# A two-layer transformer trunk: sixteen weight-sum transfers and the masks issued later, and the transposes of the second token half issued in two pieces with a free order

## The chip, the cores and the metric

The kernel runs on one core of one Trainium2 chip. The metric is device time in microseconds for one whole execution, as the median over the timed runs. The core has a matrix engine (PE, with its weight loads counted apart as PEld), a vector engine (DVE), a scalar engine (ACT), GpSimd (POOL) and a synchronisation engine (SP) that issues most transfers; POOL issues the rest. Each engine works through its own instructions in the order in which they stand in its queue, and waits where the next one lacks an operand or a buffer.

## The reference, cut to what matters

The input is 1024 tokens of 1024 channels in fp32. Each of two layers is: a SwiGLU feed-forward block (FFN) with half weight, a token mixer, a second FFN with half weight. Each block has an RMSNorm on its input and one on its output.

```
def swiglu(x, wg, wu, wd):
    return (jax.nn.silu(x @ wg) * (x @ wu)) @ wd
...
for layer in range(DEPTH):                       # DEPTH = 2
    f = swiglu(rmsnorm(h, ffn_pre_g[layer, 0]), ...)      # D_FF = 1408
    h = h + 0.5 * rmsnorm(f, ffn_post_g[layer, 0])
    m = rmsnorm(h, mix_pre_g[layer])
    m = hybrid_mixer(m, ...) if layer % 2 == 0 else stick_breaking(m, ...)
    h = h + rmsnorm(m, mix_post_g[layer])
    f = swiglu(rmsnorm(h, ffn_pre_g[layer, 1]), ...)
    h = h + 0.5 * rmsnorm(f, ffn_post_g[layer, 1])
```

## The kernel before, in words

**Stages.** `build` runs six stages in a row: the FFNs and mixers of layer 0, then those of layer 1. The four FFNs are called L0F0, L0F1, L1F0 and L1F1 here, by layer and position. Tokens are handled in two halves of 512 (`TB`). Every fp32 operand is split into a rounded high part (a cast on ACT) and a rest (a subtraction on DVE), and a product is three matmuls per 128-row block, `mm3`: high weight by high data, high weight by data rest, weight rest by high data (lines 287, 288, 289). The third of them is the first to need DVE's half of the weight split.

**The gate loop.** `gu` computes gate and up with a Strassen scheme on 2x2 blocks. Its first loop runs over the 11 column blocks c of the gate weight. For each c it loads a 128-column tile (`load_w`, tile `rawt`), splits it into two quarters `wq` (`split_w`, ACT line 336 and DVE line 337), multiplies the first quarter with the first token half (`pa`, 12 matmuls), copies that to `ph` on ACT (line 434), and later, in `a12`, adds the second quarter's 12 matmuls into the same `pa` and applies Silu (ACT, line 414). The list `second` holds the products whose second quarter is still to come.

**The second token half.** Beside the gate loop `second_half(part)` brings in the second token half: `make_raw` transposes normed tokens into `xps` (line 327, four 128x128 transposes to a tile, one from each of the four token tiles `fx`, `fo1` or `xn`) and ACT evicts them to `xr` (line 329). Four parts of two tiles each go with c = 2 to 5. `combos(j)`, with c = 4 to 7, makes the Strassen sums of them on DVE (lines 388 to 397, seven operations and three splits each). The normed tokens come from `epilogue(1, ...)` of the stage before; its last steps, on DVE, ACT and POOL in turn, are the row scales `rs` (line 234) and the scaled rows (line 248).

**The up loop.** The second loop of `gu` runs over the same 11 c with five products of 12 matmuls (`pb`, `pc`, `pd`, `pc`, `pd`). `blocks(c)` loads one gate and one up tile and makes the block differences on POOL (lines 421 to 424), which ACT and DVE then split.

**Jobs.** Strassen sums of weights that later stages need are made in DRAM by transfers that POOL issues, sixteen to a set (`Blocks.sums`, line 82): `vsum` for the mixer's value projection, `wsum` for its output projection, `dsum` for the FFN's down projection. A set is four rounds that each wait for the round before. `job(loop)` issues a few per c. In L0F0 the gate loop has the mixer's masks (`mask_steps`, lines 163 to 187) and the `vsum` set, the up loop has `dsum` and `wsum`.

**Order.** A planner sets each engine's order from its own estimate of times. Instructions given to `keep_in_program_order` (here `pin`) stay in the order of the code among themselves. The gate loop's matmuls with c below 6 and the transposes of `second_half` are pinned, and so are the jobs on POOL.

**The down stage.** `down_strassen` follows with products `da`, `db`, `dc`, `de`, `dd`; its differences on POOL are lines 715 and 725. Then come `epilogue(0, ...)`, whose `rs` are POOL's next work, `make_x` for the first token half (line 268), and `epilogue(1, ...)`. The mixer's `values` first reads `vsum` as tile `rawd`.

Of the kernel before, what the change touches and what calls it, by code (L numbers as in the profile page):

```python
# [19 lines left out]
P = 128  # L20
D = 1024
S = 1024
KD = D // P
DFF = 1408
NF = DFF // P
# [28 lines left out]
class Blocks:  # L54
# [15 lines left out]
    def sums(self, T):  # L70

        dma = self.t.nc.gpsimd.dma_start
        pin = self.t.tc.keep_in_program_order
        T1, T2, T3, T4 = (T[n] for n in (1, 2, 3, 4))
        h = slice(0, self.KH * P // 2), slice(self.KH * P // 2, self.KH * P)
        steps = []
        for dst, src, add in ((T1, self.block(0, 0), None), (T3, self.block(0, 1), None),
                              (T1, self.block(0, 1), 1), (T3, self.block(1, 1), 1), (T2, T1, None),
                              (T2, self.block(1, 1), 1), (T4, T2, None), (T4, self.block(1, 0), 1)):
            for i in h:  # L80
                def step(dst=dst, src=src, add=add, i=i):
                    pin(dma(out=dst[i], in_=src[i], accum_op=ALU.add) if add else dma(out=dst[i], in_=src[i]))
                steps.append(step)
        return steps
# [5 lines left out]
class Trunk:  # L90
# [192 lines left out]

    def mm3(self, ps, ah, al, bh, bl, first, last, more=False):
        nc = self.nc
        pin = self.pin_mm or (lambda i: i)
        pin(nc.tensor.matmul(ps, lhsT=ah, rhs=bh, start=first, stop=False, skip_group_check=more))  # L287
        pin(nc.tensor.matmul(ps, lhsT=ah, rhs=bl, start=False, stop=False, skip_group_check=more))  # L288
        pin(nc.tensor.matmul(ps, lhsT=al, rhs=bh, start=False, stop=last, skip_group_check=more))  # L289


    def load_cols(self, w, c0, n):
# [24 lines left out]
        return ps  # L317


    def make_raw(self, xns, gname, gi, pool, order=range(KD), pin=lambda i: i):  # L320

        nc = self.nc
        res = {}
        for k in order:
            ps = self.tp.tile([P, TB], F32, name="xps", tag="tp")
            for t in range(NTT):
                pin(nc.tensor.transpose(ps[:, t * P:(t + 1) * P], xns[t][:, k * P:(k + 1) * P], self.ident))
            r = pool.tile([P, TB], F32, name="xr", tag="xr")
            nc.scalar.activation(out=r, in_=ps, func=AF.Copy, scale=self.col(gname, gi * KD + k))
            res[k] = r  # L330
        return res
# [22 lines left out]
    def gu(self, cx, wg, wu, A, xn1, gname, gi, jobs, begun):  # L354


        nc = self.nc
# [3 lines left out]
        xr = self.dyn(raw, "xr", KD)  # L361
        R = {}
# [1 line left out]
        rows = {}  # L364

        def second_half(part):
            R.update(self.make_raw(xn1, gname, gi, xr, [part, part + 4], pin))
            if part < 3:
                return
            self.hctx.close()  # L370
            self.foctx.close()
            rows["sx"] = self.dyn(s4, "sx", 4, side="right")
            rows["t2"] = self.dyn(s4, "t2p", 2, side="right")
# [8 lines left out]
        def combos(j):  # L382

            a21, a22 = R[j], R[j + 4]
            hi = lambda k: A[k][:, 0].bitcast(F32)
            lo = lambda k: A[k][:, 1].bitcast(F32)
            s1 = xr.tile([P, TB], F32, name="s1", tag="s1", bufs=1)
            tt(out=s1, in0=a21, in1=a22, op=ALU.add)
            stile(1, s1)
            tt(out=a21, in0=hi(j), in1=a21, op=ALU.subtract)  # L390
            tt(out=a21, in0=a21, in1=lo(j), op=ALU.add)
            stile(3, a21)
            tt(out=s1, in0=s1, in1=hi(j), op=ALU.subtract)
            tt(out=s1, in0=s1, in1=lo(j), op=ALU.subtract)
            stile(2, s1)
            tt(out=a21, in0=hi(j + 4), in1=s1, op=ALU.subtract)
            tt(out=a21, in0=a21, in1=lo(j + 4), op=ALU.add)

        ph, second = [], []
        pin = self.tc.keep_in_program_order  # L400
        paces = 3, -(-len(jobs[1]) // NF)

        def job(loop):
            for f in jobs[loop][:paces[loop]]:
                f()
            del jobs[loop][:paces[loop]]


        def a12():

# [14 lines left out]
            return {"t1": b11, "t2": t2, "t3": b12, "t4": b21, "b22": b22}  # L425

        for c in range(NF):

            self.pin_mm = pin if c < 6 else None
            h = [self.ph.tile([P, TB], F32, name="ph%d" % tb, tag="ph") for tb in range(2)]  # L430
            w0, w1 = begun if begun and c == 0 else self.gate_weights(wg, c)
            ps = self.acc.tile([P, TB], F32, name="pa", tag="acc")
            self.quarter(ps, w0, A[0:4], True, True)
            nc.scalar.copy(out=h[1], in_=ps)
            while len(second) > (c < 8):
                a12()
            second.append((ps, w1, h))
            ph.append(h)
            if 2 <= c <= 5:
                second_half(c - 2)  # L440
            if 4 <= c <= 7:
                combos(c - 4)
            if c > 2:
                job(0)

        B = blocks(0)
        W = [self.split_w(B[n]) for n in ("t2", "t3")]
# [8 lines left out]
        for c in range(NF):  # L456
# [10 lines left out]
            last = c == NF - 1  # L467
# [26 lines left out]
            tt(out=h[1], in0=c21, in1=c22, op=ALU.mult)  # L494
            if c > NF // 2:
                self.down_sums(ph, c - 1 - NF // 2)
            job(1)
        tmp.close()
        s4.close()
        return ph  # L500
# [110 lines left out]
    def ffn(self, l, f, x0, xn1, hsrc, hdst, last):  # L611
        a = self.a
        wg, wu, wd = a["ffn_w_gate"][l, f], a["ffn_w_up"][l, f], a["ffn_w_down"][l, f]
        cx = ExitStack()
        self.ph = self.dyn(cx, "ph", 2 * NF)
        self.s1 = []

        sums = lambda *sets: [step for steps in zip(*[B.sums(T) for B, T in sets]) for step in steps]
        down = self.down_blocks(l, f), self.wd[l, f]
        jobs = [], []  # L620
        if l + f == 0:
            jobs = self.mask_steps() + sums((self.value_blocks(0), self.tv)), sums(down, (self.out_blocks(0), self.td))
        elif l == 0:
            jobs = [], sums(down, (self.value_blocks(1), self.tv))
        elif f == 0:
            jobs = [], sums(down)
        ph = self.gu(cx, wg, wu, x0, xn1, "ffn_pre_g", 2 * l + f, jobs, self.begun_w)
        self.open_fo()
        pg = self.load_pg(a["ffn_post_g"][l, f])
        nxt = ("mix_pre_g", l) if f == 0 else ("ffn_pre_g", 2 * (l + 1))  # L630
        r = self.down_strassen(wd, self.wd[l, f], ph, pg, hsrc, hdst, None if last else nxt)
        cx.close()
        self.hctx.close()
        return r
# [13 lines left out]
        gt(out=z, in0=x, in1=z, op=ALU.subtract)  # L648
        self.s1.append(s1)

    def down_strassen(self, w, T, ph, pg, hsrc, hdst, nxt):
        nc = self.nc
        tt = nc.vector.tensor_tensor
        gt = nc.gpsimd.tensor_tensor
# [68 lines left out]
            tt(out=u2[t], in0=pb[t], in1=u2[t], op=ALU.add)  # L723
        for j in range(KH):
            gt(out=ph[j + KH][0], in0=ph[j][0], in1=ph[j + KH][0], op=ALU.subtract)

        cp = [pair("c22") for _ in range(2)]
        c22 = [cp[t // 2][:, t % 2] for t in range(NTT)]
# [917 lines left out]
    def build(self):  # L1646
# [15 lines left out]
            self.normed(h, h)  # L1662
        src = a["x"][0]
        n = 0
        self.begun_w = self.pin_mm = None
        stages = [(l, step) for l in range(2) for step in ("f0", "mix", "f1")]
        firsts = [(lambda l=l: self.row_weights(lambda j: self.value_blocks(l).src(j, 0))) if step == "mix" else
                  (lambda l=l, f=int(step[1]): self.gate_weights(a["ffn_w_gate"][l, f], 0)) for l, step in stages]
# [43 lines left out]
```

## Time and profile before

| | |
|---|---|
| time, median of 3 runs | 2486.64 us (2486.34 to 2493.13) |
| time of the profiled execution | 2488.17 us |
| its span | 2486.2 us |
| PE busy | 2352.8 us, 95% of the span, 11165 matmuls and transposes |
| DVE, ACT, POOL busy | 1840.1, 1141.2, 723.4 us |
| mean clock granted to PE | 0.985 of full speed |

The profile is one execution. "Busy" counts an engine's own work, not its waits; "idle before" an instruction, with what released it, is where an engine's waits show. In the timeline a row has the start, the duration, the engine, line, operation, tiles and shapes, and in brackets the idle time just ahead of it. Matmul durations overlap: in a run of matmuls the distance between two starts is what counts.

### The profile page before, as it was taken

The numbers are of one execution on the slowest core, as the hardware profiler recorded it, in microseconds if no ns is written. First come the engines' busy times: TensorE is split into PE (matmuls) and PEld (weight loads), VectorE is DVE, ScalarE is ACT, GpSimd is POOL, SyncE is SP. The second block draws the span as 40 slices with busy tenths as digits, with TensorE's granted clock in tenths as the row PEclk, the third lists the DMA queues.
The fourth block names the chain that finished last, engine by engine and source line by source line (L and its number), as shares of the span: only waits on it lengthen the run. The fifth ranks groups of instructions, "written<-read, shape, count | busy, mean of one in ns | idle before, by whom it ended". The sixth has DMA issues, their size and how long they took to land. (4 is left out here: it accounts for less than half of the span.)

```text
span 2486.2 us, 31734 instructions
## 1 busy us (share of the span) xinstructions
PE 2352.8 (95%) x11165; PEld 1925.0 (77%) x11165; DVE 1840.1 (74%) x2877; ACT 1141.2 (46%) x2285; POOL 723.4 (29%) x729
## 2 busy tenths in 40 slices
PE   7999999999888898999989999999999999799998
PEld 6778877777677776877768878778888878588886
DVE  7768789387577778678688677785767677786777
ACT  6323456332466666423456225463333345652343
POOL 3547210011011111567022563110332430234520
PEclk9999999999999998999999999999999999899999
DMA  8867444411112463767454743355574244532234
GB/s 240 229 154 187 141 148 155 143 52 68 60 60 77 150 222 108 194 151 180 140 184 125 162 118 123 122 167 180 126 185 104 90 131 163 176 85 76 73 110 170
DMA packets 278407, 343.64 MB, mean 138 GB/s; under 512 B 13972, under 2 KB 190312, under 8 KB 277736
## 3 DMA queue, kind: packets, MB, share of 16 engines
q1 hardware_dynamic: 251352, 261.39, 33.6%
q0 software_dynamic: 26896, 80.22, 14.2%
q8 instruction: 88, 1.44, 0.2%
q14 instruction: 71, 0.58, 0.1%
HBM read 292.28 MB, written 124.78 MB: 168 GB/s over the span
## 5 line engine op out<-in xcount | busy, mean ns | idle before, releaser
L234 POOL TENSOR_TENSOR rs<-ms,nhalf 128x1 f32<-128x1 f32 (+1 forms) x136 | 103.7, 769 | 839.6 <-DVE ms L232 728.7
L336 ACT CAST wq<-rawt 128x512 fp32r<-128x512 f32 x264 | 163.3, 622 | 362.6 <-PE pc L289 181.9
L337 DVE TENSOR_TENSOR wq<-rawt,wq 128x512 fp32r<-128x512 f32 x264 | 246.5, 938 | 41.9 <-ACT wq L336 37.9
L276 ACT CAST hl<-rawd 128x512 fp32r<-128x512 f32 x212 | 130.7, 620 | 212.0 <-PE dc L289 63.9
L277 DVE TENSOR_TENSOR hl<-rawd,hl 128x512 fp32r<-128x512 f32 x212 | 155.4, 737 | 81.6 <-ACT hl L276 81.5
L287 PE MATMUL pps<-hl,wh 128*128 128x512 f32 x512 | 209.3, 409 | 1.4 <-ACT k L966 1.2
L288 PE MATMUL pps<-hl,wh 128*128 128x512 f32 x512 | 203.6, 398 | 0.0
L289 PE MATMUL pps<-hl,wl 128*128 128x512 f32 x512 | 202.9, 396 | 0.0
L421 POOL TENSOR_TENSOR rawt<-rawt 128x512 f32<-128x512 f32 x44 | 65.7, 1494 | 342.7 <-DMA rawt<-in_ffn_w_up_dram 287.0
L287 PE MATMUL pa<-hl,wq 128*128 128x512 f32 x352 | 143.1, 407 | 5.8 <-ACT wq L336 3.2
L289 PE MATMUL pa<-hl,wq 128*128 128x512 f32 x352 | 141.0, 401 | 8.1 <-DVE wq L337 8.1
L287 PE MATMUL pc<-hl,wq 128*128 128x512 f32 x336 | 133.0, 396 | 12.7 <-DVE c L472 11.8
L288 PE MATMUL pa<-hl,wq 128*128 128x512 f32 x352 | 140.5, 399 | 0.0
L289 PE MATMUL pc<-hl,wq 128*128 128x512 f32 x336 | 133.3, 397 | 0.0
L288 PE MATMUL pc<-hl,wq 128*128 128x512 f32 x336 | 133.3, 397 | 0.0
L288 PE MATMUL pd<-hl,wq 128*128 128x512 f32 x336 | 131.3, 391 | 0.0
L289 PE MATMUL pd<-hl,wq 128*128 128x512 f32 x336 | 131.2, 391 | 0.0
L287 PE MATMUL pd<-hl,wq 128*128 128x512 f32 x336 | 131.1, 390 | 0.0
L1076 DVE TENSOR_TENSOR_SCAN a<-a,zero 128x128 f32<-128x128 f32 (+3 forms) x64 | 90.2, 1409 | 46.5 <-POOL a L1073 46.2
L983 PE MATMUL z<-k,q 128*128 128x512 f32 (+2 forms) x480 | 113.6, 361 | 9.5 <-ACT k L966 4.3
L287 PEld LDWEIGHTS pps<-hl,wh 128*128 128x128 f32 x512 | 97.7, 191 | 21.5 <-ACT k L966 2.6
L289 PEld LDWEIGHTS pps<-hl,wl 128*128 128x128 f32 x512 | 97.5, 191 | 21.1
(359 smaller groups left out, 6642.0 us busy)
## 6 DMA issues: line engine op xcount, KB each, us to landing
rawt<-in_ffn_w_gate_dram SPq DMA_DIRECT2D x88, 512.0 KB, 4.0
dsum<-in_ffn_w_down_dram POOLq DMA_DIRECT2D x48, 640.0 KB, 8.0
rawt<-in_ffn_w_up_dram SPq DMA_DIRECT2D x44, 512.0 KB, 4.2
rawd<-dsum SPq DMA_DIRECT2D x80, 256.0 KB, 2.7
hres<-h SPq DMA_DIRECT2D x40, 512.0 KB, 2.7
h<-hres SPq DMA_DIRECT2D x40, 512.0 KB, 4.6
rawd<-in_ffn_w_down_dram SPq DMA_DIRECT2D x76, 256.0 KB, 2.7
dsum<-dsum POOLq DMA_DIRECT2D x16, 640.0 KB, 5.7
```

What stands on the lines that cost most here:

```text
L234: nc.gpsimd.tensor_tensor(out=rs, in0=ms, in1=self.nhalf.to_broadcast([P, n]) if n > 1 else self.nhalf, op=ALU.pow)
L276: nc.scalar.copy(out=t[:, 0], in_=src)
L277: nc.vector.tensor_tensor(out=t[:, 1], in0=src, in1=t[:, 0].bitcast(F32), op=ALU.subtract)
L287: pin(nc.tensor.matmul(ps, lhsT=ah, rhs=bh, start=first, stop=False, skip_group_check=more))
L288: pin(nc.tensor.matmul(ps, lhsT=ah, rhs=bl, start=False, stop=False, skip_group_check=more))
L289: pin(nc.tensor.matmul(ps, lhsT=al, rhs=bh, start=False, stop=last, skip_group_check=more))
L336: nc.scalar.copy(out=w[:, 0], in_=src)
L337: nc.vector.tensor_tensor(out=w[:, 1], in0=src, in1=w[:, 0].bitcast(F32), op=ALU.subtract)
L421: gt(out=b11, in0=b12, in1=b11, op=ALU.subtract)
L983: nc.tensor.matmul(z[:, :wide], lhsT=lhs[:, i * P:(i + 1) * P], rhs=rhs[:, c0:c0 + wide], start=j == 0, stop=j == len(passes) - 1 and not ...
L1076: nc.vector.tensor_tensor_scan(out=ra, data0=ra, data1=self.zero1.to_broadcast([P, n]), initial=1.0, op0=ALU.mult, op1=ALU.add)
```

## The change

Three edits in one:

1. In L0F0 the sixteen `vsum` transfers and the masks leave the gate loop. They are handed to `down_strassen` as `steps` and issued there behind POOL's last difference, transfers first and masks behind them. The gate loop has no jobs any more; the up loop's jobs are the same ones at the same pace.
2. In all four FFNs `second_half` comes in two parts of four tiles (c = 3 and 4) in place of four parts of two (c = 2 to 5), and `combos` goes with c = 5 to 8 in place of 4 to 7; the last `pa` drains one c later.
3. Nothing on PE in the gate loop is pinned, so that the planner orders these matmuls and transposes.

```
 def mm3(self, ps, ah, al, bh, bl, first, last, more=False):
-    pin = self.pin_mm or (lambda i: i)
-    pin(nc.tensor.matmul(ps, lhsT=ah, rhs=bh, ...))      # and the two others
+    nc.tensor.matmul(ps, lhsT=ah, rhs=bh, ...)
...
 def second_half(part):
-    R.update(self.make_raw(xn1, gname, gi, xr, [part, part + 4], pin))
-    if part < 3:
+    R.update(self.make_raw(xn1, gname, gi, xr, [2 * part, 2 * part + 4, 2 * part + 1, 2 * part + 5]))
+    if not part:
         return
...
-    self.pin_mm = pin if c < 6 else None
...
-    while len(second) > (c < 8):
+    while len(second) > (c < 9):
         a12()
...
-    if 2 <= c <= 5:
-        second_half(c - 2)
-    if 4 <= c <= 7:
-        combos(c - 4)
-    if c > 2:
-        job(0)
+    if c in (3, 4):
+        second_half(c - 3)
+    if 5 <= c <= 8:
+        combos(c - 5)
...
 if l + f == 0:
-    jobs = self.mask_steps() + sums((self.value_blocks(0), self.tv)), sums(down, (self.out_blocks(0), self.td))
+    jobs = sums(down, (self.out_blocks(0), self.td))
+    steps = sums((self.value_blocks(0), self.tv)) + self.mask_steps()
...
 # down_strassen
     for j in range(KH):
         gt(out=ph[j + KH][0], in0=ph[j][0], in1=ph[j + KH][0], op=ALU.subtract)
+    for f in steps:
+        f()
```

The work itself is unchanged: every engine has the same instructions, and SP's queue has the same order. What moves is the order on PE, ACT and DVE inside the four gate loops, and on POOL in L0F0.

PE in L0F1 (L1F1 has the same pattern), where the second token half comes in; `fo1_0` to `fo1_3` are its four normed token tiles, `pa` are gate products. Before:

```order
L288 MATMUL pa_8511<-hl_8383,wq_8423 128x512
L289 MATMUL pa_8511<-hl_8383,wq_8423 128x512
L327 MATMUL xps_8586<-ident_98,fo1_0_8386 128x128
L327 MATMUL xps_8586<-ident_98,fo1_1_8387 128x128
L327 MATMUL xps_8586<-ident_98,fo1_2_8388 128x128
L327 MATMUL xps_8586<-ident_98,fo1_3_8389 128x128
L327 MATMUL xps_8593<-ident_98,fo1_0_8386 128x128
```

And after:

```order
L288 MATMUL pa_8596<-hl_8351,wq_8590 128x512
L326 MATMUL xps_8623<-ident_98,fo1_0_8386 128x128
L326 MATMUL xps_8630<-ident_98,fo1_0_8386 128x128
L326 MATMUL xps_8637<-ident_98,fo1_0_8386 128x128
L326 MATMUL xps_8644<-ident_98,fo1_0_8386 128x128
L286 MATMUL pa_8661<-hl_8327,wq_8655 128x512
L287 MATMUL pa_8661<-hl_8327,wq_8655 128x512
L326 MATMUL xps_8623<-ident_98,fo1_1_8387 128x128
L326 MATMUL xps_8630<-ident_98,fo1_1_8387 128x128
L326 MATMUL xps_8637<-ident_98,fo1_1_8387 128x128
L326 MATMUL xps_8644<-ident_98,fo1_1_8387 128x128
L288 MATMUL pa_8661<-hl_8327,wq_8655 128x512
```

Before, 48 gate matmuls stand between the stage's first `pa` and the first transpose, and that transpose's tile needs all four token tiles at once. After, 75 stand there, and the transposes go by token tile, with 2, 3 and 4 matmuls between the tiles.

PE at the start of L0F0; `wq_310` and `wq_313` are the two quarters of gate block c = 0, `wq_334` the first quarter of c = 1, `pa_316` and `pa_340` their products. Before:

```order
L289 MATMUL pa_316<-hl_244,wq_310 128x512
L287 MATMUL pa_340<-hl_235,wq_334 128x512
L288 MATMUL pa_340<-hl_235,wq_334 128x512
L289 MATMUL pa_340<-hl_235,wq_334 128x512
L287 MATMUL pa_340<-hl_238,wq_334 128x512
```

And after:

```order
L288 MATMUL pa_316<-hl_244,wq_310 128x512
L286 MATMUL pa_316<-hl_247,wq_313 128x512
L287 MATMUL pa_316<-hl_247,wq_313 128x512
L288 MATMUL pa_316<-hl_247,wq_313 128x512
L286 MATMUL pa_316<-hl_250,wq_313 128x512
L287 MATMUL pa_316<-hl_250,wq_313 128x512
L288 MATMUL pa_316<-hl_250,wq_313 128x512
L286 MATMUL pa_316<-hl_253,wq_313 128x512
L286 MATMUL pa_340<-hl_235,wq_334 128x512
L287 MATMUL pa_340<-hl_235,wq_334 128x512
L287 MATMUL pa_316<-hl_253,wq_313 128x512
```

The second quarter of c = 0 now begins ahead of block c = 1, and the two interleave.

POOL in L0F0, where the `vsum` set ends and the up loop's first block follows (`vsum_135` is the last of the four sums). Before:

```order
L82 DMA vsum_135<-vsum_133 16x8192 x2
L82 DMA vsum_135<-in_hyb_w_in_dram 256x512 x2
L421 TENSOR_TENSOR rawt<-rawt 128x512
L422 TENSOR_TENSOR t_890<-rawt 128x512
L423 TENSOR_TENSOR rawt<-rawt 128x512
L424 TENSOR_TENSOR rawt<-rawt,t_890 128x512
L82 DMA dsum_1_140<-in_ffn_w_down_dram 320x512
```

And after, in the down stage:

```order
L720 TENSOR_TENSOR ph_746<-ph_456,ph_746 128x512
L82 DMA vsum_132<-in_hyb_w_in_dram 256x512 x2
L82 DMA vsum_134<-in_hyb_w_in_dram 256x512 x2
L82 DMA vsum_132<-in_hyb_w_in_dram 256x512 x2
L82 DMA vsum_134<-in_hyb_w_in_dram 256x512 x2
L82 DMA vsum_133<-vsum_132 16x8192 x2
L82 DMA vsum_133<-in_hyb_w_in_dram 256x512 x2
L82 DMA vsum_135<-vsum_133 16x8192 x2
L82 DMA vsum_135<-in_hyb_w_in_dram 256x512 x2
L168 MEMSET zero_2407 128x1
```

The block differences of c = 0 now stand right behind the input norms' `rs`, and the set stands behind the last difference of the down stage, ahead of the masks and of `epilogue(0)`'s `rs`.

More of the change, by code (lines that the diff above doesn't have):

```diff
@@ L285, in mm3 @@
         nc = self.nc
-        pin = self.pin_mm or (lambda i: i)
-        pin(nc.tensor.matmul(ps, lhsT=ah, rhs=bh, start=first, stop=False, skip_group_check=more))
-        pin(nc.tensor.matmul(ps, lhsT=ah, rhs=bl, start=False, stop=False, skip_group_check=more))
-        pin(nc.tensor.matmul(ps, lhsT=al, rhs=bh, start=False, stop=last, skip_group_check=more))
+        nc.tensor.matmul(ps, lhsT=ah, rhs=bh, start=first, stop=False, skip_group_check=more)
+        nc.tensor.matmul(ps, lhsT=ah, rhs=bl, start=False, stop=False, skip_group_check=more)
+        nc.tensor.matmul(ps, lhsT=al, rhs=bh, start=False, stop=last, skip_group_check=more)
     def load_cols(self, w, c0, n):
@@ L317, in proj, with make_raw @@
         return ps
-    def make_raw(self, xns, gname, gi, pool, order=range(KD), pin=lambda i: i):
+    def make_raw(self, xns, gname, gi, pool, order=range(KD)):
         nc = self.nc
@@ L326, in make_raw @@
             for t in range(NTT):
-                pin(nc.tensor.transpose(ps[:, t * P:(t + 1) * P], xns[t][:, k * P:(k + 1) * P], self.ident))
+                nc.tensor.transpose(ps[:, t * P:(t + 1) * P], xns[t][:, k * P:(k + 1) * P], self.ident)
             r = pool.tile([P, TB], F32, name="xr", tag="xr")
@@ L399, in gu, with job @@
         ph, second = [], []
[L400 to L404, printed above, removed]
+        pace = -(-len(jobs) // NF)
+        def job():
+            for f in jobs[:pace]:
                 f()
-            del jobs[loop][:paces[loop]]
+            del jobs[:pace]
         def a12():
@@ L496, in gu @@
                 self.down_sums(ph, c - 1 - NF // 2)
-            job(1)
+            job()
         tmp.close()
@@ L619, in ffn @@
         down = self.down_blocks(l, f), self.wd[l, f]
-        jobs = [], []
+        jobs, steps = [], []
         if l + f == 0:
-            jobs = self.mask_steps() + sums((self.value_blocks(0), self.tv)), sums(down, (self.out_blocks(0), self.td))
+            jobs = sums(down, (self.out_blocks(0), self.td))
+            steps = sums((self.value_blocks(0), self.tv)) + self.mask_steps()
         elif l == 0:
-            jobs = [], sums(down, (self.value_blocks(1), self.tv))
+            jobs = sums(down, (self.value_blocks(1), self.tv))
         elif f == 0:
-            jobs = [], sums(down)
+            jobs = sums(down)
         ph = self.gu(cx, wg, wu, x0, xn1, "ffn_pre_g", 2 * l + f, jobs, self.begun_w)
@@ L630, in ffn @@
         nxt = ("mix_pre_g", l) if f == 0 else ("ffn_pre_g", 2 * (l + 1))
-        r = self.down_strassen(wd, self.wd[l, f], ph, pg, hsrc, hdst, None if last else nxt)
+        r = self.down_strassen(wd, self.wd[l, f], ph, pg, hsrc, hdst, None if last else nxt, steps)
         cx.close()
@@ L649, in down_sums, with down_strassen @@
         self.s1.append(s1)
-    def down_strassen(self, w, T, ph, pg, hsrc, hdst, nxt):
+    def down_strassen(self, w, T, ph, pg, hsrc, hdst, nxt, steps):
         nc = self.nc
@@ L1664, in build @@
         n = 0
-        self.begun_w = self.pin_mm = None
+        self.begun_w = None
         stages = [(l, step) for l in range(2) for step in ("f0", "mix", "f1")]
```

## The prediction

> **What bounds the kernel now.** I read the busy times first, then PE's list of waits, then the timeline where those waits lie.
>
> ```profile
> PE 2352.8 (95%) x11165; PEld 1925.0 (77%) x11165; DVE 1840.1 (74%) x2877; ACT 1141.2 (46%) x2285; POOL 723.4 (29%) x729
> ```
>
> PE is the bound, and the work on it is unchanged. An edit can win time only from PE's idle time, 133.4 us of the span of 2486.2 (2486.2 less 2352.8), and from stretches in which matmuls run slowly. PE's longest waits, over the whole program (us in all, times, longest):
>
> ```profile
> PE xps L327 <- DVE ms L232: 16.7, 6, 5.6
> PE pc L287 <- DVE c L472: 11.8, 7, 4.4
> PE pa L289 <- DVE wq L337: 8.1, 3, 5.5
> ```
>
> All three are in loops that the change reorders. The first is the entry of the second token half in L0F1 and L1F1. PE's timeline in L0F1 (start, us):
>
> ```profile
> 949.64 0.39 PE L289 MATMUL pa<-hl,wq 128*128 128x512 f32 x1
> 955.67 0.45 PE L327 MATMUL xps<-ident,fo 128*128 128x128 f32 x1 [5.64 <-DVE ms L232]
> 957.44 0.48 PE L327 MATMUL xps<-ident,fo 128*128 128x128 f32 x1 [1.32 <-DVE ms L232]
> 959.29 0.47 PE L327 MATMUL xps<-ident,fo 128*128 128x128 f32 x1 [1.38 <-DVE ms L232]
> 961.15 1.33 PE L327 MATMUL xps<-ident,fo 128*128 128x128 f32 x5 [1.38 <-DVE fo L248]
> 962.13 0.78 PE L287 MATMUL pa<-hl,wq 128*128 128x512 f32 x1
> ...
> 965.97 0.40 PE L287 MATMUL pa<-hl,wq 128*128 128x512 f32 x1
> ```
>
> The 48 gate matmuls are used up at 949.64; then PE stands before four transposes, each waiting for one more normed token tile: 5.64 + 1.32 + 1.38 + 1.38 = 9.72 us. The nine matmuls from 962.13 to 965.97 take 3.84 us, 0.427 each, where undisturbed ones start 0.2275 apart (949.64 closes an undisturbed run): 1.8 us more. So 11.5 us go here. The three waits on `ms` are 8.34 us, and twice that is the 16.7 of the whole program, so L1F1 loses as much.
>
> **Edits 2 and 3 in L0F1 and L1F1.** DVE's rows that make the four tiles ready, the first and the last of the four (the two between start at even distances of 1.85):
>
> ```profile
> 954.78 0.75 DVE L248 TENSOR_SCALAR fo<-h,rs 128x1024 f32<-128x1024 f32 x1
> 960.34 0.75 DVE L248 TENSOR_SCALAR fo<-h,rs 128x1024 f32<-128x1024 f32 x1 [0.44 <-POOL rs L234]
> ```
>
> The tiles are ready at 955.53, 957.38, 959.23 and 961.09, and DVE's order ahead of them stays. The changed order has 75 matmuls ahead of the first transpose, 27 more: 949.87 + 27 x 0.2275 = 956.0. Each tile then feeds four transposes (0.1 us each, from the eight in 0.8 us that start at 35.30, below). Tile 0 finds no wait; 2 matmuls later, at 956.9, PE waits 0.5 for tile 1; after 3 more 0.7 for tile 2; after 4 more 0.6 for tile 3. PE ends at 961.5 with 84 matmuls and 16 transposes done. Before, it had 48 and 8 done at 962.1. The surplus of 36 matmuls and 8 transposes is 8.2 + 0.8 us, plus the 0.6 by which PE is there sooner, plus the 1.8 of slow matmuls: 11.4 us. Two of the matmuls between the tiles need a DVE split that stands among the scales; I take off 1.9 for that and for whatever the shorter waits cost: 9.5 us each, with 11.4 as the upper end. The lower end is 0: if DVE ends the loop later than PE (rival below), PE returns all of it.
>
> The Trainium skill, "TensorE: Matmul & The Clock Gate", section on the HAM clock gate, says that an idle window of about 3.4 us halves the clock and that as much busy time restores it. The trace agrees: 0.427 us per matmul behind the 5.64. By that rule the waits of at most 0.7 would leave the clock alone, which is what the sum takes from the rows; if they did not, 1.8 of each 9.5 would stay lost.
>
> **Edit 3 at the start of L0F0.** Timeline of PE, then the ACT and DVE rows that it hangs on:
>
> ```profile
> 19.34 0.39 PE L289 MATMUL pa<-hl,wq 128*128 128x512 f32 x1
> 22.92 0.50 PE L287 MATMUL pa<-hl,wq 128*128 128x512 f32 x1 [3.19 <-ACT wq L336]
> 24.75 0.80 PE L289 MATMUL pa<-hl,wq 128*128 128x512 f32 x1 [1.10 <-DVE wq L337]
> ...
> 30.47 0.43 PE L287 MATMUL pa<-hl,wq 128*128 128x512 f32 x1
> 35.30 1.03 PE L327 MATMUL xps<-ident,fx 128*128 128x128 f32 x8
> ```
>
> ```profile
> 20.68 0.64 ACT L434 COPY ph<-pa 128x512 f32<-128x512 f32 x1
> 28.48 2.77 DVE L337 TENSOR_TENSOR wq<-rawt,wq 128x512 fp32r<-128x512 f32 x4
> ```
>
> PE loses 3.19 + 1.10 idle, and 13 matmuls at 0.427 until 30.47 (5.72 us instead of 2.96): 2.76. Together 7.1. After, the second quarter of c = 0 comes next; it needs only the copy, which ends at 21.32: a wait of 21.32 - 19.57 = 1.75. Behind it 0.4 for the rest of c = 1 and 1.27 for that of c = 2, the first of DVE's four splits (29.17, against 27.9): 3.4 in three pieces. The gain is 7.1 - 3.4 = 3.7; take 3.7, with 0.9 as the lower end (the slow stretch stays) and 5.6 as the upper.
>
> **Edit 1: POOL free in L0F0.** Waits between 36 and 90 us, and POOL's and PE's entries into the up loop, L0F0 and L0F1:
>
> ```profile
> ACT wq L336 <- POOL t L422: 6.9, 1, 6.9
> PE pa L287 <- ACT ph L434: 1.3, 2, 0.7
> ```
>
> ```profile
> 78.97 1.61 POOL L421 TENSOR_TENSOR rawt<-rawt 128x512 f32<-128x512 f32 x1
> 996.17 1.29 POOL L421 TENSOR_TENSOR rawt<-rawt 128x512 f32<-128x512 f32 x1 [35.86 <-DMA rawt<-in_ffn_w_up_dram]
> ```
>
> ```profile
> 89.78 0.39 PE L287 MATMUL pb<-hl,wq 128*128 128x512 f32 x1
> 1015.63 0.39 PE L287 MATMUL pb<-hl,wq 128*128 128x512 f32 x1
> ```
>
> In L0F0 POOL begins the first block differences when the last `vsum` transfer is out, 10.8 us ahead of `pb`; in L0F1, where no set stands there, 19.5 us ahead. ACT sits 6.9 us behind that late difference, and the two copies that PE waits for stand behind ACT: 1.3 us, gone when POOL is early (0 to 1.3; take 1.3). The up loops of the two, as PE's waits from 90 to 166 and from 1016 to 1160:
>
> ```profile
> PE pc L287 <- DVE c L472: 6.3, 2, 4.4
> ```
>
> ```profile
> PE pc L287 <- DVE c L472: 2.7, 2, 1.5
> ```
>
> Both loops have the same number of transfers per c, so the shorter lead is the likely source of the extra 3.6 us. I expect a lead near L0F1's, but not all of it, since up loads and combinations crowd there: 3.0 (from -2, if the later combinations make DVE late, to 6.3). The lead in L0F1 and L1F1 shrinks a little, since PE comes sooner: -1.0 (-3 to 0).
>
> The Trainium skill, "GPSIMD Engine Reference", sections Specifications and Key points, says that POOL shares its memory interface with VectorE and that operations with two such inputs contend; it speaks against moving POOL's differences among DVE's combinations. The trace shows it:
>
> ```profile
> 996.21 3.49 DVE L337 TENSOR_TENSOR wq<-rawt,wq 128x512 fp32r<-128x512 f32 x2
> ```
>
> Two splits beside POOL take 3.49 us, four alone at 28.48 took 2.77: 1.05 more each. A block of four POOL operations (about 6 us) thus costs DVE some 4 us. The next table shows DVE idle for 13 of 46 us in that loop, which covers it; uncovered, it would take the 3.0 away.
>
> **Edit 1: the down stage.** POOL's rows of the masks, the set and the hole:
>
> ```profile
> 27.42 0.10 POOL L168 MEMSET zero<- 128x1 f32 x1
> 36.92 2.46 POOL L82 DMA_DIRECT2D vsum<-in_hyb_w_in_dram  x4
> 333.31 2.33 POOL L234 TENSOR_TENSOR rs<-ms,nhalf 128x1 f32<-128x1 f32 x3 [65.64 <-DVE ms L232]
> ```
>
> Masks take 36.92 - 27.42 = 9.5, the set 78.97 - 36.92 = 42.05, waits on landings included. The hole in front of `epilogue(0)`'s `rs` is 65.64, which leaves 14 us. Behind the set on POOL are only the masks and that `rs`; DVE's scales, and PE's transposes of the first half, wait for it only once the 14 us are gone, and then a microsecond costs one. For the DMA engines I use three stretches (length, then busy us of PE, PEld, DVE, ACT, POOL, then clock, DMA share, GB/s): with the set, the down stage, and L0F1's like loop without a set.
>
> ```profile
> 36.00:82.00 46.00, 46.00 (x219) 38.34 (x217) 33.01 (x53) 26.07 (x48) 15.22 (x21) 1.00 1.02 250
> 268.00:325.00 57.00, 57.00 (x253) 47.16 (x253) 36.28 (x58) 27.40 (x52) 0.00 (x0) 1.00 0.41 129
> 962.00:1014.00 52.00, 52.00 (x236) 43.16 (x235) 41.94 (x60) 32.02 (x58) 15.58 (x14) 0.96 0.38 109
> ```
>
> The set adds 1.02 - 0.38 = 0.64 of 46 us, 29 us. The down stage has 0.41 x 57 = 23 us, so 52 of 57 would be taken: full, not over. Loads there, and the gate loads beside the set (KB each, median us to landing):
>
> ```profile
> rawd<-dsum SPq DMA_DIRECT2D x15, 256.0 KB, 2.7
> ```
>
> ```profile
> rawt<-in_ffn_w_gate_dram SPq DMA_DIRECT2D x5, 512.0 KB, 11.3
> ```
>
> The code issues a down load four products ahead, 4 x 12 x 0.2275 = 10.9 us. A `rawd` of half the bytes beside the set should land in 5.7 to 11.3. Cost 0; up to -3 if some land at the upper end.
>
> L1F0 holds the other two of the three waits on `wq` (8.1 - 1.1 = 7.0). They hang on DVE finishing the stage before; the order there does not change that: 0, between -2 and 2.
>
> **Sum.** 9.5 + 9.5 + 3.7 + 1.3 + 3.0 - 1.0 = 26.0 us. The profiled execution took 2488.17 (2486.2 of it span) and would take 2462.2; the median run is 1.5 below it, so the median goes from 2486.64 to 2460.6.
>
> **Rivals.**
> - *DVE takes PE's place in the second half.* From 962 to 1014 DVE is busy for 41.94 of 52 us; if PE needs 42, DVE has nothing left, and the combinations now start one c later. Then both 9.5 come back as waits ahead of `pb`, and 26.0 - 19 = 7.0 remain: 2479.6. Against it: DVE's operations of that stretch include splits for matmuls behind `pb`, and since all four token tiles are ready at 961.09 as before, the combinations can begin at the same time; only PE comes sooner.
> - *No net change.* A free order rests on the planner's estimates; each gap that it fills may open another where an estimate is off by a microsecond, as the splits between the tiles might. Some 26 us of new waits would be needed, in four loops 6.5 each: 2486.6. Nothing in the rows shows such waits.
> - *Slower: the set starves the down stage.* Four loads in flight carry PE as long as each lands in 10.9 us. At 20 us a product takes 5.0 instead of 2.73, and the 57 us become 105: 2460.6 + 48 = 2508. It outweighs the gains from about 10.9 x (57 + 33.5) / 57 = 17 us per load on. For it: 11.3 at 512 KB with the engines full. Against: 52 of 57, half the bytes.
>
> **How the numbers follow.** The summed case gets 0.71, with its own range 2449 to 2471 (the 9.5s at 11.4 and L0F0's terms at their upper ends; or the lower ends of the L0F0 terms and half of one 9.5). DVE as the bound gets 0.14, no net change 0.08, slower 0.07. About 0.3%, 7.5 us, is what a measurement of this kernel can tell from no change, so faster means below 2479.2. Of DVE's 0.14 I count 0.10 as faster, since a part of the 9.5s would survive. That makes 0.81 faster, 0.12 same, 0.07 slower. The range 2447 to 2480 leaves out the last two cases and little else.
>
> **What the changed profile would show.** PE's wait on `ms` at the transposes falls from 16.7 to about 4, none over 1.5 us, with full clock behind them. Between 19 and 30 us no wait over 2 us and no slow stretch. POOL's first difference in L0F0 starts 15 us or more ahead of `pb`, and `pc` waits for DVE there for 3 us or less. In the down stage the `vsum` set lies between 268 and 325, PE stays without waits, and `rs` follows at its old distance. I am wrong if `pb` of L0F1 or L1F1 has a DVE wait of several microseconds ahead of it, if `da` to `dd` wait on `rawd`, or if `rs` comes late.

## The result and the profile after

The changed kernel takes 2460.62 us (median of 4 runs, 2457.76 to 2466.01) against 2486.49 before (median of 4). The ratio is 0.9893, with a 95% interval of 0.9869 to 0.9918: about 26 us less. The profiled execution took 2459.79 us, 2458.0 of it span. In its rows line numbers are a few lower than before: 286 to 288 are the three matmuls, 326 the transposes, 418 to 421 POOL's differences, 462 and 465 the first two additions of an up-loop block, 486 and 487 its last two products, 336 DVE's split. In the experiments they shift again by a few lines; the tiles tell which one is meant. With edit 2 alone and with edit 3 alone one run took over 3300 us, and so did one run of the kernel before that was timed with them; their medians and ratios here leave these runs out.

The busy times, then the two of the three waits shown before that are still high in PE's list (us, times, longest):

```profile
PE 2347.3 (95%) x11165; PEld 1920.1 (78%) x11165; DVE 1842.9 (75%) x2877; ACT 1136.5 (46%) x2285; POOL 738.0 (30%) x729
```

```profile
PE pc L286 <- DVE c L465: 11.8, 8, 3.0
...
PE xps L326 <- DVE ms L232: 7.1, 5, 5.2
```

PE's work is the same, so the 28.2 us of span are idle time (22.7 less) and slow matmuls (5.5 less busy). The wait for `ms` at the transposes fell from 16.7 to 7.1, and of that 5.2 is a single wait in L1F0. The wait for DVE's `wq` is no longer among the longest; in L1F0, where it was 7.0, PE now waits those 5.2. The wait of `pc` for DVE is as large as before, and this is where the predicted sum was not quite what happened. The entry of the second token half in L0F1, PE's timeline:

```profile
949.91 0.66 PE L326 MATMUL xps<-ident,fo 128*128 128x128 f32 x4 [0.73 <-DVE ms L232]
951.77 0.66 PE L326 MATMUL xps<-ident,fo 128*128 128x128 f32 x4 [0.23 <-DVE ms L232]
953.62 0.66 PE L326 MATMUL xps<-ident,fo 128*128 128x128 f32 x4 [0.28 <-DVE fo L248]
954.04 0.47 PE L286 MATMUL pa<-hl,wq 128*128 128x512 f32 x1
954.35 0.39 PE L287 MATMUL pa<-hl,wq 128*128 128x512 f32 x1
```

Where 9.72 us were idle there are 1.24, and the matmuls behind start 0.23 to 0.31 apart, not 0.427. The start of L0F0:

```profile
21.35 0.50 PE L286 MATMUL pa<-hl,wq 128*128 128x512 f32 x1 [1.75 <-ACT ph L429]
24.75 0.50 PE L288 MATMUL pa<-hl,wq 128*128 128x512 f32 x1 [0.16 <-DVE ms L232]
28.91 0.50 PE L288 MATMUL pa<-hl,wq 128*128 128x512 f32 x1 [0.65 <-DVE wq L336]
```

The waits of 3.19 and 1.10 and the slow stretch are replaced by 1.75 + 0.16 + 0.65 = 2.6 us at full clock. To see what each stage gained I take, from each profile's timeline, the starts of the first `pa`, the first `pb` and the first `da` of each FFN. From `pa` to `pb` is the gate loop, from `pb` to `da` the up loop (L0F0 before: 16.59, 89.78 and 250.99, so 73.19 and 161.21).

| gate loop / up loop, us | L0F0 | L0F1 | L1F0 | L1F1 |
|---|---|---|---|---|
| before | 73.19 / 161.21 | 78.21 / 154.58 | 73.61 / 156.36 | 77.38 / 151.36 |
| after (all three edits) | 67.05 / 159.52 | 66.88 / 158.80 | 72.71 / 153.00 | 67.11 / 153.40 |
| edit 1 alone | 71.01 / 154.19 | 77.50 / 154.83 | 72.47 / 154.13 | 78.97 / 151.36 |
| edits 2 and 3 | 76.38 / 157.38 | 66.99 / 162.23 | 71.42 / 156.40 | 66.36 / 153.40 |
| edit 3 alone | 74.75 / 163.66 | 66.81 / 158.48 | 72.08 / 156.06 | 66.87 / 152.53 |
| edit 2 alone | 75.48 / 162.78 | 71.90 / 158.29 | 73.62 / 154.14 | 71.75 / 151.36 |
| edits 1 and 3 | 67.22 / 161.84 | 66.79 / 160.66 | 71.71 / 152.18 | 67.18 / 152.52 |
| no POOL differences | 101.17 / 151.36 | 86.89 / 151.37 | 74.68 / 151.36 | 66.37 / 151.35 |

The rows below "after" are experiments. Later experiments leave some of these loops as the changed kernel has them; in their profiles its gate loops of L0F0, L0F1 and L1F1 repeat within 0.9 us and the up loops within 1.5. L0F0's up loop also differs by 2.2 us between two runs with the same code there (161.84 with edits 1 and 3, 159.61 in a later run). L1F0's up loop repeats only within 3 us (153.00, 153.63, 156.00), so the 3.4 us that the table shows there are not claimed for the change.

### The profile page after: what moved, and what is told of

Same layout as the page of the kernel before. It is cut to its first block, busy times and chain, and to the rows that moved or that the text cites. A ratio compares the mean times of both kernels' runs of the same rounds, so it can differ in the third digit from the quotient of the medians.

```text
span 2458.0 us, 31746 instructions
## 1 busy us (share of the span) xinstructions
PE 2347.3 (95%) x11165; PEld 1920.1 (78%) x11165; DVE 1842.9 (75%) x2877; ACT 1136.5 (46%) x2285; POOL 738.0 (30%) x729
## 5 line engine op out<-in xcount | busy, mean ns | idle before, releaser
L418 POOL TENSOR_TENSOR rawt<-rawt 128x512 f32<-128x512 f32 x44 | 79.7, 1810 | 362.5 <-DMA rawt<-in_ffn_w_up_dram 283.3
L286 PE MATMUL pc<-hl,wq 128*128 128x512 f32 x336 | 133.2, 396 | 12.6 <-DVE c L465 11.8
L286 PE MATMUL pa<-hl,wq 128*128 128x512 f32 x352 | 140.3, 399 | 2.6 <-ACT ph L429 2.2
L288 PE MATMUL pa<-hl,wq 128*128 128x512 f32 x352 | 138.9, 396 | 0.8 <-DVE wq L336 0.7
L287 PE MATMUL pa<-hl,wq 128*128 128x512 f32 x352 | 138.5, 394 | 0.0
L288 PEld LDWEIGHTS pps<-hl,wl 128*128 128x128 f32 x512 | 97.2, 190 | 20.8
```

What stands on the lines that cost most here:

```text
L418: gt(out=b11, in0=b12, in1=b11, op=ALU.subtract)
```

## What the experiments asked

The gate loops of L0F1 and L1F1 gained 11.3 and 10.3 us, but their up loops gave 4.2 and 2.0 of that back. My theory was that the free order makes the gain in L0F1 and L1F1, that edit 1 only takes POOL and ACT out of PE's way in L0F0, and that edit 2's later combinations cause the new wait. The rivals: that edit 1 or edit 2 carries more of it, and that the new wait is the price of PE arriving earlier, whoever brings that about.

**The three edits apart.** Edit 1 alone is the kernel before with the set and the masks handed to the down stage:

```
-    jobs = self.mask_steps() + sums((self.value_blocks(0), self.tv)), sums(down, ...)
+    jobs = [], sums(down, ...)
+    steps = sums((self.value_blocks(0), self.tv)) + self.mask_steps()
```

> Edit 1 alone: the set and the masks move to the down stage, pins and four pieces stay. Theory (the gain sits in the order on PE, and edit 1 only frees POOL, ACT and the DMA engines in L0F0): the two copy waits of 1.3 us in L0F0's gate loop go and its up loop is 1 to 3 us shorter; L0F1, L1F0, L1F1 as before, with 16.7 us of waits for ms at the transposes; in all 2 to 4 us less, 2482 to 2485, so hardly to be told from no change. Rival (the gain in L0F0 is mostly edit 1's, since the set's traffic slows the first loads): 6 to 8 us less, with the wait of 3.19 at 22.9 us gone.

Measured: 2475.91 us, ratio 0.9949 (0.9929 to 0.9968). About 10 us (8 to 18 by the interval), more than either size I had given. The stages come from its slowest execution, 2481.52 us, so they show less than the median does: L0F0's up loop fell by 7.0, its gate loop by 2.2, while the wait of 3.3 at its start stayed. POOL's first difference stands at 68.26 there, 19.5 us ahead of `pb`, and PE's waits in that up loop, 6.6 for DVE before, are:

```profile
PE pc L287 <- DVE c L472: 1.8, 3, 1.2
```

So edit 1 is worth much more in the up loop than the 3.0 I gave it, as long as PE does not come sooner as well. That the lead alone is worth this is not shown: the set's traffic is gone from the gate loop, too (DMA share 0.38 between 36 and 82 us, where it was 1.02). The other half, edits 2 and 3, keeps `jobs` as before:

> Edits 2 and 3 with the set and the masks left in L0F0's gate loop. Theory: all of the change but 2 to 4 us: 2462 to 2466; gate loops of L0F1 and L1F1 10 to 11.5 us shorter than before, L0F0's start 3.7 us shorter. Rival (with the set in the gate loop, the combinations that come one c later and POOL's late first difference meet, so the free order pays back in L0F0): pb of L0F0 waits 3 us or more for DVE or POOL and the whole is above 2468.

Measured: 2466.32 us, ratio 0.9922 (0.9909 to 0.9935). The size is the theory's, and so are L0F1's and L1F1's gate loops (11.2 and 11.0 less). But in L0F0 the rival holds: the gate loop is 3.2 us longer than before. PE's timeline just ahead of its `pb`:

```profile
87.76 0.79 PE L286 MATMUL pa<-hl,wq 128*128 128x512 f32 x1 [6.25 <-ACT ph L433]
```

ACT is behind, as it was before (it waits 10.7 us for POOL's `t`, 6.9 before), and POOL's first difference comes at 79.83, late as before; PE now reaches that place sooner and waits 6.25 us, with 2.6 us of half clock behind it. With the set in the gate loop, edits 2 and 3 gain 0.6 us in the whole of L0F0 (233.8 against 234.4), for all that its start is some 4 us better.

Edit 3 alone drops the pins and nothing else:

```
-    pin(nc.tensor.matmul(...))            # and the transposes of second_half
+    nc.tensor.matmul(...)
```

> Edit 3 alone: nothing pinned on PE, but four pieces of two tiles from c = 2 on and combinations from c = 4 on. In the compiled order 71 matmuls stand ahead of the first transpose in L0F1 and L1F1, with 5, 4 and 3 between the token tiles. Theory (the free order does it, the pieces only set how many transposes each step holds): gate loops of L0F1 and L1F1 9 to 11 us shorter than before, L0F0's start 3.7 us shorter, in all 20 to 25 us less, 2461 to 2467; and if the late combinations of edit 2 cause the new wait of 2.8 us ahead of the second pc in L0F1, that wait is absent here. Rival (both edits are needed): less than 12 us.

Measured: 2471.16 us, ratio 0.9932 (0.9907 to 0.9956). By the median that is less than expected, though the interval, 11 to 23 us less, reaches into the 20 to 25. For its stages a second profile was taken:

> Edit 3 alone once more, for its trace. The wait of 2.70 to 2.86 us for DVE ahead of L0F1's second pc stands in the whole change, in edits 2 and 3, and in edit 2 alone, not in the kernel before and not in edit 1 alone. Theory (it comes with edit 2, whose larger pieces and later combinations leave DVE no pause before pb): absent here, L0F1's up loop 154 to 156 us. Rival (it comes with PE being 8 to 11 us earlier at pb, whatever the cause): present here too, up loop 158 us or more. L0F1's gate loop 67 to 69 us in both.

That execution took 2473.15 us. L0F1's and L1F1's gate loops are 66.81 and 66.87, as short as with all three edits. What is missing is in L0F0, 4.0 us longer than before. And the rival on the new wait holds: L0F1's up loop is 158.48, with a wait of 2.01 us for DVE and 1.6 of slow matmuls in its first block. Edit 2 is not its cause.

Edit 2 alone keeps the pins:

> Edit 2 alone: two pieces of four tiles from c = 3 on, combinations one c later, order still held. 72 matmuls stand ahead of the first transpose, but all sixteen then stand together and the first tile needs all four token tiles. Theory: the 24 more matmuls cover 5.5 us, the rest of the wait (about 5, in pieces below 2 us) stays, and the slow stretch of 1.8 goes: L0F1 and L1F1 6 to 7.5 us shorter each, L0F0's start unchanged with its 3.19 wait; in all 11 to 15 us less, 2471 to 2476. Rival (what counts is only that the transposes stand later): as much as the whole change in L0F1 and L1F1, 10 us each, 2465.

Measured: 2476.51 us, ratio 0.9959 (0.9943 to 0.9975). The gate loops of L0F1 and L1F1 are 6.3 and 5.6 shorter, as reckoned for 24 more matmuls, but L0F0 is 3.9 us longer and L0F1's up loop 3.7: about 9 us in all by the medians (6 to 14 by the interval) instead of 11 to 15. Last, edits 1 and 3 without 2:

> Edits 1 and 3 without edit 2 (four pieces of two tiles from c = 2, combinations from c = 4, nothing pinned, the set and the masks in the down stage). Gate and up loop together were, before, 234.4 in L0F0, 232.8 in L0F1, 228.7 in L1F1; edit 1 alone took L0F0 to 225.2, edit 3 alone took L0F1 and L1F1 to 225.3 and 219.4, and all three edits stand at 226.6, 225.7 and 220.5. Theory (edit 1 makes the gain in L0F0 and edit 3 that in L0F1 and L1F1; edit 2 adds nothing): 225 to 227, 225 to 226 and 219 to 221, the whole 2458 to 2463. Rival (the larger pieces are needed for part of it): 4 us or more above the changed kernel, 2465 and up.

Measured: 2459.75 us, ratio 0.9898 (0.9869 to 0.9927), the changed kernel's time. The gate loops are the changed kernel's, too; L0F0 and L0F1 in all came out at 229.1 and 227.5, some 2 us above my ranges, which for L0F0 is no more than its scatter, and other stages lower. At the level of the whole the larger pieces add nothing that can be told.

**What gives the time back.** In the changed kernel's L0F1, just ahead of the up loop, POOL, DVE and PE:

```profile
977.61 9.06 POOL L418 TENSOR_TENSOR rawt<-rawt 128x512 f32<-128x512 f32 x1 [24.83 <-DMA rawt<-in_ffn_w_up_dram]
```

```profile
984.85 0.68 DVE L393 TENSOR_TENSOR s<-s,hl 128x512 f32<-128x512 f32 x1
988.72 1.11 DVE L336 TENSOR_TENSOR wq<-t,wq 128x512 fp32r<-128x512 f32 x1 [3.19 <-ACT wq L335]
989.76 1.80 DVE L395 TENSOR_TENSOR xr<-hl,s 128x512 f32<-128x512 f32 x1
991.48 1.78 DVE L277 TENSOR_TENSOR hl<-s,hl 128x512 fp32r<-128x512 f32 x1
```

```profile
1008.04 0.47 PE L286 MATMUL pc<-hl,wq 128*128 128x512 f32 x1 [2.83 <-DVE c L465]
```

Before, POOL's first difference came when DVE's combinations were over, and took 1.29 us. Now it falls among them and takes 9.06: it ends at 986.67, 1.1 us after DVE's unbroken run of operations of 0.68, which is about the time that it takes by itself. Then DVE waits 3.19 for the split of the second difference, `t`, and its next operations take 1.8 beside the rest of POOL's work. PE arrives and waits 2.83. I took away the differences of the first two blocks:

```
 def blocks(c):
     ...
+    if c < 2:
+        return {"t1": b11, "t2": b22, "t3": b12, "t4": b21, "b22": b22}
```

> The changed kernel without POOL's differences of blocks 0 and 1 in the four FFNs (8 of 44 operations of each of lines 418 to 421; the blocks are used as loaded). Theory (at L0F1's entry into the up loop DVE's unbroken run holds POOL's first difference off for 9.06 us where it took 1.29 before, and the differences beside it then stretch DVE's operations from 0.69 to about 1.78): without them DVE has no idle 3.19 there, its operations keep 0.69, the wait of 2.83 and the slow 1.65 behind it go, and L0F1's up loop falls from 158.8 to 153 to 155; in all four loops together 5 to 10 us less than the changed kernel. Rival (DVE's own work is too much for the shorter loop): the wait stays at 2 us or more.

One execution: 2453.46 us. The wait in L0F1's first block is gone, but the up loop is 157.71, only 1.1 shorter: a wait of 2.83, with the same slow stretch, now stands at 1058.73, in a later block. PE's list for that up loop is the changed kernel's to the digit (4.2, 2, 2.8):

```profile
PE pc L286 <- DVE c L467: 4.2, 2, 2.8
```

DVE's rows ahead of that later wait:

```profile
1051.80 1.11 DVE L336 TENSOR_TENSOR wq<-t,wq 128x512 fp32r<-128x512 f32 x1 [3.48 <-ACT wq L335]
1052.83 1.78 DVE L488 TENSOR_TENSOR ph<-ph,c 128x512 f32<-128x512 f32 x1
```

So the contention is real at the first place, and the wait that is left has the same form: POOL starts that block only at 1048.46, DVE stands 3.48 for the split of `t`, and its two products, which stand ahead of the additions, take 1.78 and 1.77. The other loops say more than L0F1. All four together are 616.8 us against 624.7, 7.9 less and within the theory's 5 to 10, though L0F0 and L1F0 scatter by 2 to 3 us. L1F1's up loop, which repeats within 0.02 us, is back at 151.36 without a wait, although PE enters it as early as in the changed kernel (gate loop 67.60). In L1F1 the first two blocks of POOL's differences are thus the whole loss of 2.0. In L0F1 a held-off first difference isn't even needed for the wait. With edit 2 alone POOL's first difference comes among the combinations, too:

```profile
990.18 1.85 POOL L421 TENSOR_TENSOR rawt<-rawt 128x512 f32<-128x512 f32 x1 [28.70 <-DMA rawt<-in_ffn_w_up_dram]
```

It isn't held off there; DVE's next four operations take 1.77 to 1.78 instead, and PE still waits 2.70. I tried DVE's order next: in each later block two products stand ahead of the additions for which PE waits. They were put behind them and held there, and the two additions were held in order with them:

```
-    tt(out=h[0], in0=h[0], in1=c12, op=ALU.mult)      # and h[1]; in the same block
+    late.append(...)                                  # run behind the next block's c22 addition, pinned
```

> The changed kernel with DVE's last two products of each up-loop block c (lines 486 and 487) put behind the next block's two additions (lines 462 and 465), for which PE waits, and held there. Theory (what the gate loops gain comes back as waits of pc for DVE, since these two products, 0.69 us each alone and 1.78 beside POOL, stand ahead of the additions): the waits at the second pc of the later blocks go (3.0 and 1.3 us with 1.6 of slow clock in L0F0, 0.8 and 1.4 in L0F1, 1.0 in L1F0, 1.8 in L1F1), the one in L0F1's first block (2.8) stays; 5 to 10 us less than the changed kernel, 2450 to 2455. Rival (POOL's late differences hold DVE up, not its order): less than 2 us.

Measured: 2474.96 us, ratio 0.9958 (0.9944 to 0.9972), 14 us slower than the changed kernel. PE's list says what happened; over the whole program:

```profile
PE pd L286 <- DVE c L482: 19.2, 18, 3.2
...
PE pc L286 <- DVE c L466: 4.8, 3, 2.9
```

The waits of `pc` shrank from 11.8 to 4.8, and 19.2 us of waits of `pd` took their place, since the products now stand ahead of the next addition. The rival was nearer, and even it expected no loss. The last experiment on this left out all of POOL's differences:

> The changed kernel without any of POOL's block differences in the up loops (all 44 operations of each of lines 418 to 421 left out, the blocks used as loaded); loads, splits, DVE's additions and POOL's transfers stay. Eleven blocks of 60 matmuls take 150.2 us at 0.2275; L1F1's up loop without any wait took 151.4 before the change. Theory (what the up loops lose above that, 8.1 in L0F0, 7.4 in L0F1, 1.6 in L1F0 and 2.0 in L1F1, is POOL's: its differences come late and stretch DVE's operations beside them): all four at 151 to 152.5, no wait of pc for DVE above 0.5 us, the whole 15 to 19 us under the changed kernel, 2441 to 2446. Rival (DVE's own work, or loads that land late, set the loop): waits of 1 us and more stay in at least two loops, less than 10 us.

Measured: 2495.19 us, ratio 1.0036, so the time is a miss. The up loops are the theory's: 151.36, 151.37, 151.36 and 151.35, with no wait of PE in any of the four that the list of waits shows. Two cautions go with that. With no differences between them, POOL issues the up loop's transfers early, from 26.27 us on in L0F0, so in three of the loops both are gone at once. And in L0F0 and L0F1 the gate loops are 34 and 20 us longer than in the changed kernel, so PE enters the up loop late, which could by itself remove the waits. Only L1F1, which has no transfers and a gate loop of 66.37, shows the differences alone (153.40 to 151.35). The early transfers also cost the time. Waits of all engines from 15 to 117 us:

```profile
DVE lmul L201 <- DMA lp<-in_diff_lambda_dram: 41.3, 1, 41.3
...
PE pa L286 <- ACT ph L411: 31.3, 1, 31.3
```

DVE stands 41.3 us in front of a tiny operation whose load is caught among the transfers (it lands in 31.6 us where it took 3.7); combinations and PE stand behind it.

**L0F0 in smaller pieces.** The changed kernel with four pieces and the earlier combinations in L0F0 alone:

> The changed kernel with four pieces from c = 2 and combinations from c = 4 in L0F0 alone, where the normed tokens are ready early; nothing is pinned. Theory (in L0F0 edit 2 gives back what edit 1 wins, 154.2 us of up loop with edit 1 alone against 159.5 with all three): L0F0's up loop 153 to 156, its gate loop 67 to 68, and the whole 4 to 6 us under the changed kernel, 2454 to 2457. Rival (the longer up loop comes from PE's free order or from chance): 159 again, no change from 2460.

Measured: 2461.24 us, ratio 0.99 (0.9882 to 0.9918). L0F0 is 67.23 and 159.61, no different. Here, too, the pieces do not matter.

**The cover in the down stage.** The changed kernel's POOL rows and loads there:

```profile
258.21 1.61 POOL L720 TENSOR_TENSOR ph<-ph,ph 128x512 f32<-128x512 f32 x1 [0.69 <-DVE hl L277]
305.82 0.42 POOL L168 MEMSET zero<- 128x1 f32 x1
325.21 2.86 POOL L234 TENSOR_TENSOR rs<-ms,nhalf 128x1 f32<-128x1 f32 x3 [9.63 <-DVE ms L232]
```

```profile
rawd<-dsum SPq DMA_DIRECT2D x15, 256.0 KB, 7.1
```

```profile
260.00:317.00 57.00, 57.00 (x253) 47.20 (x252) 36.51 (x59) 27.39 (x52) 19.68 (x41) 1.00 0.98 277
```

The set takes 46 us, the masks 10, and 9.63 of the hole are left; loads land in 7.1 us instead of 2.7, the DMA engines are 0.98 busy, and PE is busy for all of the 57 us. To see whether that cover has an edge, the set was issued twice:

```
-    steps = sums((self.value_blocks(0), self.tv)) + self.mask_steps()
+    steps = sums((self.value_blocks(0), self.tv)) + sums((self.value_blocks(0), self.tv)) + self.mask_steps()
```

> The changed kernel with the sixteen vsum transfers issued twice, one set behind the other, in the down stage; the masks behind both. Theory (the set is free only as long as it ends ahead of epilogue(0)'s rs, 9.6 us of which are left): the second set takes some 40 to 46 us, rs comes 30 to 36 us late, and PE, whose transposes of the first half wait for it, loses that: the stretch from da to the mixer's first product goes from 142.3 to 170 to 178 us, the whole to 2488 to 2496. Loads of rawd still land within 10.9 us, so the products da to dd do not wait. Rival 1 (PE has dd to do meanwhile, so rs is not on its path): less than 10 us. Rival 2 (the loads starve): waits of da to dd for rawd, over 40 us lost.

One execution: 2491.03 us. POOL's `rs` and PE:

```profile
356.58 2.29 POOL L234 TENSOR_TENSOR rs<-ms,nhalf 128x1 f32<-128x1 f32 x3
```

```profile
360.41 0.76 PE L286 MATMUL dd<-hl 128*128 128x512 f32 x1 [26.28 <-DVE fo L747]
```

`rs` is 31.4 us later than in the changed kernel, PE stops for 26.28 in the middle of `dd`, and the stretch from `da` to the mixer's first product is 173.83 where it was 142.34. The products do not wait for `rawd`. The cover has the edge where the row of idle time put it.

**A try at more.** L1F0's second half one c later, against its wait of 5.17:

```
-    if c in (3, 4):
-        second_half(c - 3)
+    d = c - (gi == 2)                 # L1F0 only; combos likewise
+    if d in (3, 4):
+        second_half(d - 3)
```

> The changed kernel with the second token half and the combinations one c later in L1F0 alone, where PE still waits 5.17 us at the first transposes and runs at half clock behind it (2.56). In the compiled order 97 gate matmuls then stand ahead of the first transpose, where it was 31. Theory (PE lacks work in front of the late tiles): the wait goes, but two shorter ones appear, about 2.5 for DVE's split of c = 2 and 1.3 for ACT's copy; L1F0's gate loop 69 instead of 72 to 73, the whole 2 to 4 us less, if its up loop (151 to 156) returns nothing. Rival (as in L0F0, what PE gains ahead of pb it waits in the up loop): gate loop 69, up loop longer by the same, no change.

Measured: 2464.43 us, ratio 0.992 (0.9897 to 0.9942), not better. Two rows of PE in that gate loop:

```profile
1283.44 0.80 PE L288 MATMUL pa<-hl,wq 128*128 128x512 f32 x1 [5.90 <-DVE wq L336]
1345.85 0.80 PE L286 MATMUL pa<-hl,wq 128*128 128x512 f32 x1 [5.10 <-ACT ph L429]
```

The matmuls put ahead of the tiles need DVE splits that stand among the tiles' own steps, and a second wait opens at the end of the gate loop: 80.79 instead of 72.71. No version that clearly beats the changed kernel was found.

## Why the prediction was right

The total, 2460.6, is the measured one, and the main step, the entry of the second token half, is the one that made most of the gain. That the total agrees to a tenth is luck: the other terms erred against each other, and 4.3 of the 28.2 us come from L1F0, which was forecast at nothing.

| term | predicted gain | measured |
|---|---|---|
| gate loops of L0F1 and L1F1 | 9.5 + 9.5 | 11.3 + 10.3 |
| their up loops | -1.0 | -4.2 - 2.0 |
| L0F0's gate loop (start 3.7, copies 1.3) | 5.0 | 6.1 |
| L0F0's up loop | 3.0 | 1.7, inside the loop's scatter of 2.2 |
| L1F0 | 0 | 4.3, 3.4 of it within the loop's own scatter |
| all else (down stages, mixers, end) | 0 | 0.8 |
| sum, profiled spans | 26.0 | 28.2 |

- **The entry of the second half** went as reckoned, token tile by token tile: the upper end of 11.4 was the better number, since no wait of PE for a split among the scales shows.
- **The step that was mis-sized** is "the lead in L0F1 and L1F1 shrinks a little": -1.0 taken, -3 as its lower end, -6.2 measured. The rival on DVE was right in kind, though the waits came behind `pb` and not ahead of it, and had 29% of its size (6.2 of 21.6). I read DVE's idle time in the window and asked only whether its own work fits. What I did not ask is where POOL's first differences fall once PE and the loads come 10 us sooner: beside DVE's combinations and splits, where each of the two engines is slowed by the other. For L1F1 the runs show that this is the cause; for L0F1 they show it at the first block, and the rest is argued from rows of the same form.
- **L0F0** came out at 7.8 us against 8.0, by wrong shares. Edit 3's 3.7 at the start is real on PE (with edit 3 alone PE is 3.7 us ahead at the 200th gate matmul), but edit 1 alone already gives 9.2 us in L0F0, and edits 2 and 3 without it 0.6. What PE wins at the start it waits again around the entry of the up loop, for POOL, ACT and DVE; the terms do not add.
- **The down stage** at no cost was right, with DMA engines at 0.98 where I had 52 of 57 (0.91), and landings of 7.1 us inside the 5.7 to 11.3.
- **The lead of POOL** in L0F0 grew to 20.8 us, as foretold, but `pc` still waits 4.8 us for DVE where I had 3 or less. Edit 1 alone has 19.5 us of lead and 1.8 of waits while PE keeps its old pace; a lead of that size is not enough when PE comes earlier too. Whether the up loop's remaining loss in L0F0 is POOL's, by its differences or by the transfers that they pace, stays open.
- **Two signs missed.** Besides these 4.8 us, the wait for `ms` is 7.1 and not about 4, with one of 5.2 in L1F0 where none was to pass 1.5.
- **The range of the summed case** does not come out of its terms: the ends that are named give 2451.6 and 2474.5, not 2449 and 2471. The measured time lies inside either.

## What to carry to other kernels

When a change makes the bound engine arrive earlier somewhere, follow the others to that place too: who must have finished by then, and which of their operations now overlap that did not before. Gains of edits in one loop do not add when another engine sets that loop's end; a table of stage lengths, each edit alone, shows it quickly. A hole in an engine's queue could here be filled at no cost within its measured idle time; in the one run that went beyond it, each microsecond of overrun cost about one.

## What the runs showed of the hardware

**Half clock after less than 2 us.** I had taken waits below 2 us as safe, since one of 1.85 in the kernel before, at 100.11, had no slow stretch behind it. With edits 1 and 3, and with edits 2 and 3:

```profile
1051.65 0.47 PE L286 MATMUL pc<-hl,wq 128*128 128x512 f32 x1 [1.95 <-DVE c L471]
1051.96 0.43 PE L287 MATMUL pc<-hl,wq 128*128 128x512 f32 x1
1052.19 0.63 PE L288 MATMUL pc<-hl,wq 128*128 128x512 f32 x1
1052.62 0.63 PE L286 MATMUL pc<-hl,wq 128*128 128x512 f32 x1
```

```profile
1013.91 0.47 PE L286 MATMUL pc<-hl,wq 128*128 128x512 f32 x1 [2.86 <-DVE c L471]
1014.22 0.39 PE L287 MATMUL pc<-hl,wq 128*128 128x512 f32 x1
1014.45 0.40 PE L288 MATMUL pc<-hl,wq 128*128 128x512 f32 x1
```

A wait of 1.95 us was followed by matmuls 0.43 apart for about 3.4 us (granted clock 0.50), one of 2.86 by none (granted clock 1.00). The kernel before already had a case that I overlooked, with eight matmuls 0.43 apart behind it:

```profile
1480.19 0.47 PE L287 MATMUL pc<-hl,wq 128*128 128x512 f32 x1 [1.87 <-DVE c L472]
```

Length alone does not decide: with the products later, one wait of 3.18 us (at 215.14) has a slow stretch behind it and another of 3.18 (at 1133.68) has none. So a wait of 1.9 to 3.2 us may or may not cost another 1.6 us or more. The Trainium skill, "TensorE: Matmul & The Clock Gate", section on the HAM clock gate, states a window of about 3.4 us that runs freely. That equal waits differ in their effect agrees with that. Its rule that the clock drops after one idle window does not hold as a lower bound here, and the measurement decides.

**POOL and DVE hold each other off.** The same difference in L0F1 took 1.29 us where it started just ahead of DVE's operation (996.17 against 996.21), and 9.06 within DVE's unbroken run (8.84 to 9.06 in eight profiles with a free order). DVE's 0.69 became 1.78 to 1.80 beside POOL. Which of the two has to wait is not settled by an unbroken run alone: with edit 2 alone the difference took 1.85 in a run that the trace shows as unbroken, too, and DVE's operations were the ones that became longer. The Trainium skill, "GPSIMD Engine Reference", section Specifications, names the shared interface; the runs add that either side can pay.
